# The forget gate of a hybrid decoder block: one accumulation for two blocks of positions, advanced beside the second half's operands

## Chip, cores and metric

One Trainium2 chip, one core of it. The metric is device time in microseconds (us) for one launch of the whole layer; lower is better. The core's engines are TensorE (PE, with its weight loads shown apart as PEld), VectorE (DVE), ScalarE (ACT), GpSimd (POOL) and SyncE (SP), which issues the DMAs. Each engine executes its own list of instructions strictly in order.

## What is computed

One layer over 2048 positions of width 1024, in float32. The part that the change touches is the low-rank forget gate of the gated linear attention (GLA):

```python
h = rmsnorm(x, norm1_g)
proj = h @ w_in                                  # 3088 columns
p_q, p_k, p_v, p_g, p_a, c_b, c_c, c_h = split(proj)
gate_logits = p_a @ w_gate_up + b_gate           # p_a: 16 columns, w_gate_up: 16 x 256
log_a = log_sigmoid(gate_logits) / 16
o = gla_chunked(q, k, v, log_a)                  # chunked, with a recurrent state
o = rmsnorm(o, gla_norm_g) * silu(p_g)
o_conv = c_b * causal_conv3(c_c * c_h)
x = x + concat([o, o_conv]) @ w_out
x = x + (silu(h2 @ w_ffn_gate) * (h2 @ w_ffn_up)) @ w_ffn_down      # h2 = rmsnorm(x)
out = rmsnorm(x, norm_f_g)
```

## The kernel before

**Blocks and halves.** The 2048 positions are four blocks of 512; two blocks make a half. Nearly all matrix work goes by half, as Strassen-Winograd products: the operand of a half is a 2 x 2 arrangement (rows of the width 1024 in two halves of four tiles of 128, columns the two blocks of positions), with the seven operands `B11, T1, T2, B21, T3, B22, T4` of `PRODUCTS`. `B11` and `B21` are the two width halves of the first block, `B22` is the second width half of the second block, and `T1 = B12 - B11`, so that `B11 + T1` is the first width half of the second block.

**Split numbers.** Each float32 operand is split into a high and a low part (`split`, lines 145 to 147: a copy on ACT writes the rounded high part, a subtraction on DVE the low part), and a product takes three matmuls (`product_step`, lines 334 to 336). A `unit` (line 340) is seven products of 4 x 3 matmuls on one weight tile. For it, `unit_weights` builds seven weight quarters `wq` (seven splits, four POOL operations, four buffers). Three of its accumulators are copied out by ACT (`copied`, line 354) and three products are added on DVE (`plus`, line 358).

**Input projection.** `in_proj(half)` runs twelve units: four for k, q and v, two for the output gate (their results go through Silu on ACT, line 390), six for the convolution. For the first half the first unit is done apart, by `build_first`, while the operands are being built.

**Background work.** After each product `tick` is called. While `hurry` is set, each tick takes a `step` of the list `background`; otherwise every second tick does, and of the others every second one takes a step of `ahead`, if there is one. Before, the first half's background is, in this order: `gate_weights`, six pauses, `row_stats(2)`, `row_stats(3)`, `gate(0)`, then `unhurried`, which ends the hurry, and `h1_ahead`, which makes the second half's split operands (`h` on DVE, `t` on POOL, `hi` on ACT, `lo` on DVE, stores `si...`). `gla_half(0)` is appended after the Silu units. These calls say in which order the work is written down; a scheduler then places the instructions of each engine by its own estimate of when each is ready, so what an engine really executes is the list in the built program.

**The gate before.** `gate(half)` computes the 16 gate columns for each block apart: 16 matmuls for the first block (`B11`, `B21`: two operands, four tiles, high and low) and 24 for the second (`B11`, `T1`, `B22`), line 517, each into a bank `a_ps` of its own that ACT copies to `a_sb` (line 523). `forget_gate` then does, for each of two halves of the 256 gate columns, a float32 matmul `z` (line 533), Abs on ACT (538), a DVE operation (539), Exp and Ln on ACT (540, 541), a subtraction and four scans on DVE (542, 545), two small Exp on ACT (548, 550), a subtraction on DVE (549) and a store to `s_d`, which `gla_load` reads.

**ACT's function tables.** Exp and Ln come from one table set, Silu from another. A change of set is an instruction of its own on ACT, ACT_TABLE_LOAD. The kernel asks for the set with both Exp and Ln at the start (line 988) and in `gla_half` (line 601, ordered behind the last Silu). Elsewhere a load is put in by the compiler, ahead of an activation whose function the set in place does not have.

Of the kernel before, what the change touches and what calls it, by code (L numbers as in the profile page):

```python
# [10 lines left out]
F32 = mybir.dt.float32  # L11
F32R = mybir.dt.float32r
U32 = mybir.dt.uint32
AF = mybir.ActivationFunctionType
# [33 lines left out]
def tile_hymba_block(ctx, tc, x, xt, win, wa, wgu, wout, wffn, wdown, wdown_first, small, out):  # L48
# [33 lines left out]
    dve.memset(eps[:], EPS)  # L82
    sml = const.tile([P, N_SMALL], F32, name="sml")
    nc.sync.dma_start(sml[:], small)
    wgu_sb = mixer.tile([P, 256], F32, name="wgu_sb")
    wa_sb = mixer.tile([P, (KD + 1) * 64], F32R, name="wa_sb")
    dve.memset(wa_sb[:, KD * 64 :].bitcast(F32), 0.0)
    scores = mixer.tile([P, HEADS, P], F32, name="scores")
    dve.memset(scores[:], 0.0)
    carry = mixer.tile([P, HEADS, P], F32, name="carry")  # L90
# [34 lines left out]
    def col(c):  # L125
        return sml[:, c : c + 1]

    def bank(name="mm"):
        return ps.tile([P, PB], F32, name=name, tag="mm")
# [4 lines left out]
    def bt(name, shape=(P, PB)):  # L134
        return bx[0].tile(list(shape), F32, name=name, tag="b")

    def load(dst, src):
        return nc.sync.dma_start(dst, src)

    def store(dst, src):  # L140
        return nc.sync.dma_start(dst, src)
# [3 lines left out]
    def split(src, hi, lo):  # L145
        last_hi[:] = [act.activation(hi, src, AF.Copy)]  # L146
        return dve.tensor_tensor(lo, src, hi.bitcast(F32), ALU.subtract)  # L147
# [46 lines left out]
    def unhurried():  # L194
        hurry.clear()
        yield

    def pause(n):
        for _ in range(n):
            yield  # L200
# [194 lines left out]
    def row_stats(b):  # L395
        ssq = mtiny.tile([P, PT, 2], F32, name="ssq", tag="ssq")

        def fetch(t):
            xs = [bt("xn") for _ in range(2)]
            for e, xn in enumerate(xs):  # L400
                r0 = b * PB + t * P
                load(xn[:], x[r0 : r0 + P, e * PB : (e + 1) * PB])
            return xs

        nxt = fetch(0)
        yield
        for t in range(PT):
            xs = nxt
            if t + 1 < PT:
                nxt = fetch(t + 1)  # L410
            for e, xn in enumerate(xs):
                act.activation(xn[:], xn[:], AF.Square, accum_out=ssq[:, t, e : e + 1])
            yield
        dve.tensor_tensor(ssq[:, :, 0], ssq[:, :, 0], ssq[:, :, 1], ALU.add)
        rb = bt("rb2")
        act.activation(rb[:], rows_rstd(ssq)[:], AF.Copy)
        store(s_rb[b][:], rb[:])
# [45 lines left out]

    def gate_weights():

        raw = bt("wa", (P, KD, 32))
        load(raw[:], wa)
        w = wa_sb[:, 0 : KD * 64].rearrange("p (k e c) -> p k e c", e=2, c=32)
        split(raw[:], w[:, :, 0, :], w[:, :, 1, :])
        yield  # L470

    def build_h():
# [7 lines left out]
    def h1_ahead():  # L480

        rb = []
        for j in range(2):
            r = tiny.tile([P, PB], F32, name="rb2", tag="rb")
            load(r[:], s_rb[2 + j][:])
            rb.append(r)

        def put(n, k, h):
            hi, lo = [bx[0].tile([P, PB], F32R, name=e, tag="b") for e in ("hi", "lo")]
            split(h[:], hi[:], lo[:])  # L490
            for e, y in enumerate((hi, lo)):
                store(s_h1[n][k][:, e, :], y[:].bitcast(F32))

        yield from combine(lambda k, j: xt[2 + j, :, k, :], C_G1, rb, put)
# [12 lines left out]
    def gate(half, ops):  # L507


        for j, names in enumerate((("B11", "B21"), ("B11", "T1", "B22"))):  # L510
            a = bank("a_ps")
            for i, n in enumerate(names):
                k0 = 4 if n in ("B21", "B22") else 0
                for k in range(4):
                    w = wa_sb[:, (k0 + k) * 64 : (k0 + k) * 64 + P]
                    for e in range(2):
                        pe.matmul(  # L517
                            a[:], w, ops[n][k][:, e, :], start=(i, k, e) == (0, 0, 0),
                            stop=i == len(names) - 1 and k == 3 and e == 1,
                            skip_group_check=True,  # L520
                        )
            a_sb = bt("a_sb")
            act.activation(a_sb[:], a[:], AF.Copy)
            yield
            yield from forget_gate(2 * half + j, a_sb)

    def forget_gate(b, a_sb):
        em, dn, el = [
            mtiny.tile([P, 2, PT], F32, name=n, tag=n, bufs=4) for n in ("em", "dn", "el")
        ]  # L530
        for i in range(2):
            z = bank("z")
            pe.matmul(
                z[:], wgu_sb[0:64, i * P : (i + 1) * P], a_sb[0:64, :], start=True, stop=True
            )
            bg = col(C_BG + i)
            t1, t2 = bt("g1"), bt("g2")
            act.activation(t1[:], z[:], AF.Abs, bias=bg)
            dve.tensor_scalar(t2[:], z[:], bg, 0.0, ALU.add, ALU.min)
            act.activation(t1[:], t1[:], AF.Exp, scale=-1.0)  # L540
            act.activation(t1[:], t1[:], AF.Ln, bias=one_t)
            dve.tensor_tensor(t2[:], t2[:], t1[:], ALU.subtract)
            for t in range(PT):
                s = slice(t * P, (t + 1) * P)
                dve.tensor_tensor_scan(t1[:, s], ones[:], t2[:, s], 0.0, ALU.mult, ALU.add)
            bs = t1.rearrange("p (a b) -> p a b", b=P)
            dd = t2.rearrange("p (a b) -> p a b", b=P)
            act.activation(em[:, i, :], bs[:, :, 63], AF.Exp, scale=1.0 / 16.0)
            dve.tensor_tensor(dd, bs, bs[:, :, 63:64].to_broadcast([P, PT, P]), ALU.subtract)
            act.activation(el[:, i, :], dd[:, :, P - 1], AF.Exp, scale=1.0 / 16.0)  # L550
            dve.tensor_tensor(dn[:, i, :], em[:, i, :], el[:, i, :], ALU.mult)
            store(s_d[b][i][:], t2[:])
            yield
        decays[b] = em, dn, el

    def in_proj(half, ops, first):
        def units():
# [103 lines left out]
    def gla_outputs(b, t, kq, kt, v, g):  # L661
        first = b == 0 and t == 0
        _, dn, el = decays[b]
        o = ps.tile([P, HEADS, P], F32, name="o_ps", tag="mm")
        for h in range(HEADS):
            pe.matmul(o[:, h, :], scores[:, h, :], v[:, h, :], start=True, stop=first)
            if not first:
                pe.matmul(o[:, h, :], kq[:, 2 + h // 2, :], carry[:, h, :], start=False, stop=True)
        if b < NB - 1 or t < PT - 1:
            kv = ps.tile([P, 2, P], F32, name="kv", tag="mm")  # L670
            for i in range(2):
                for e in range(2):
                    pe.matmul(
                        kv[64 * e : 64 * e + 64, i, :], kt[:, i, 64 * e : 64 * e + 64],
                        v[:, 2 * i + e, :], start=True, stop=True,
                    )
            for i in range(2):
                last = el[:, i, t : t + 1]
                if first:
                    dve.tensor_scalar(state[i][:], kv[:, i, :], last, None, ALU.mult)  # L680
                else:
                    kvs = mtiny.tile([P, P], F32, name="kvs", tag="kvs")
                    dve.tensor_scalar(kvs[:], kv[:, i, :], last, None, ALU.mult)
                    dve.scalar_tensor_tensor(
                        state[i][:], state[i][:], dn[:, i, t : t + 1], kvs[:], ALU.mult, ALU.add
                    )
        ssq, l, y0 = [mtiny.tile([P, HEADS], F32, name=n, tag=n) for n in ("hsq", "hl", "hy")]
        sq = mtiny.tile([P, P], F32, name="sq", tag="rep")
        for h in range(HEADS):
            act.activation(sq[:], o[:, h, :], AF.Square, accum_out=ssq[:, h : h + 1])  # L690
        dve.tensor_scalar(ssq[:], ssq[:], 1.0 / P, EPS, ALU.mult, ALU.add)
        rsqrt(ssq[:], ssq[:], l[:], y0[:])
        osb = bt("osb", (P, HEADS, P))
        rs = ssq[:].rearrange("p (h c) -> p h c", c=1).to_broadcast([P, HEADS, P])
        dve.tensor_tensor(osb[:], o[:], rs, ALU.mult)
        return osb, g
# [237 lines left out]
    def last_unit(src, ops, b12, y, ssq):  # L934
# [49 lines left out]
        for j in range(2):  # L984
# [2 lines left out]

    act.preload_act_table_set("natural_log_exp_and_others")
    first_loads()
    load(wgu_sb[:], wgu)  # L990
    ops, first = build_h()
    hurry.append(True)
    background.extend(
        [
            gate_weights(), pause(6), row_stats(2), row_stats(3), gate(0, ops), unhurried(),
            h1_ahead(),
        ]
    )
    in_proj(0, ops, first)
    drain_background(lambda: len(background) < 2)  # L1000
    ops = load_pairs(s_h1)
    background.append(gate(1, ops))
# [121 lines left out]
```

## Time and profile before

| | |
|---|---|
| median of 3 runs | 2141.64 us (2137.0 to 2144.77) |
| the profiled execution | 2147.18 us, of which its span is 2145.4 us |
| mean granted TensorE clock | 0.983 of full speed |
| busy, share of the span | PE 96%, PEld 77%, DVE 67%, ACT 47%, POOL 46% |
| first half's gate matmuls (line 517) | 118 to 136 us |
| first half's Silu | 155 to 191 us |
| second half's gate matmuls | from 472 to 503 us |

Times in the views are microseconds from the start of the span. A row of a timeline gives start, duration, engine, line, operation, output and inputs, count, and in brackets the idle time of the engine just before it with what ended that. A row of groups gives count, busy time, mean nanoseconds of one, and the idle time before them. Rows of windows give busy time and instruction count of each engine in a stretch. Neighbouring instructions of one engine overlap a little in the records, so a duration is somewhat longer than the distance to the next start.

### The profile page before, as it was taken

The page shows a single profiled execution, that of the slowest core. Times are in us where ns is not written, and L with a number is a line of the kernel's source. Part 1 is how long each engine was busy: PE and PEld are TensorE (multiplying, and loading weights), DVE is VectorE, ACT ScalarE, POOL GpSimd, SP SyncE. Part 2 cuts the span into 40 slices and gives each one's busy share as a digit, 9 for nine tenths or more (in the row PEclk, how much of TensorE's full clock was granted, in tenths as well). Part 3 has the DMA queues.
Part 4 walks back from the last instruction along what each step waited for, and adds up shares of the span by engine and source line. Part 5 has one row for each costly group of instructions (what it writes and reads, how often), then busy time and mean ns, then how long its engine had stood idle before and what let it go on. Part 6 is the DMA issues. An engine that isn't in the chain of part 4 may idle for free.

```text
span 2145.4 us, 26958 instructions
## 1 busy us (share of the span) xinstructions
PE 2052.6 (96%) x9137; PEld 1658.6 (77%) x9137; DVE 1438.1 (67%) x2035; ACT 1008.4 (47%) x1961; POOL 983.5 (46%) x707
## 2 busy tenths in 40 slices
PE   6899899999999999999999999999999999999996
PEld 4677787887788887788888887787888888887774
DVE  7668975548664496688887674654686677664554
ACT  6455345564544334554555453333464454553344
POOL 3425422221201374555655436774644654435773
PEclk9899999999999999999999999999999999999998
DMA  7348667432486982466454577688455455587662
GB/s 270 125 145 296 225 267 249 154 121 88 154 305 190 348 295 103 167 246 220 181 226 177 208 303 266 257 333 351 155 199 210 148 188 196 186 334 275 265 265 108
DMA packets 191563, 471.85 MB, mean 220 GB/s; under 512 B 20032, under 2 KB 65344, under 8 KB 181824
## 3 DMA queue, kind: packets, MB, share of 16 engines
q1 hardware_dynamic: 191424, 470.12, 60.5%
q8 instruction: 72, 1.18, 0.2%
q14 instruction: 67, 0.55, 0.1%
HBM read 301.22 MB, written 168.82 MB: 219 GB/s over the span
## 4 chain that ended last, share of the span: by engine, by line
PE 73%; DMA 10%; DVE 10%; issue 3%; ACT 3%; POOL 1%; SPq 0%; DVEq 0%; ACTq 0%; POOLq 0%
PE mm L334 21%; PE mm L336 21%; PE mm L335 21%; DVE wq L147 2%; PE mm L742 2%; PE mm L745 2%; PE mm L743 2%; DMA raw<-in_wdown_dram 1%; DVE op L147 1%; DMA op<-sa_B 1%; DVE h L460 1%; DMA op<-shT 1%; DMA raw<-in_wffn_dram 1%; PE a_ps L517 1%; DVE so L147 1%
## 5 line engine op out<-in xcount | busy, mean ns | idle before, releaser
L334 PE MATMUL mm<-op,wq 128*128 128x512 f32 x2495 | 987.4, 398 | 31.1 <-ACT c L354 17.0
L336 PE MATMUL mm<-op,wq 128*128 128x512 f32 x2495 | 971.7, 394 | 19.6 <-DVE wq L147 18.8
L335 PE MATMUL mm<-op,wq 128*128 128x512 f32 x2495 | 979.0, 392 | 2.6 <-DVE op L147 2.6
L147 DVE TENSOR_TENSOR wq<-raw,wq 128x512 fp32r<-128x512 f32 (+2 forms) x628 | 532.2, 852 | 306.7 <-ACT wq L146 304.9
L146 ACT ACTIVATE wq<-raw 128x512 fp32r<-128x512 f32 (+2 forms) x628 | 367.7, 589 | 582.1 <-PE mm L336 416.0
L334 PEld LDWEIGHTS mm<-op,wq 128*128 128x128 f32 x2495 | 473.2, 190 | 151.2 <-ACT c L354 22.9
L336 PEld LDWEIGHTS mm<-op,wq 128*128 128x128 f32 x2495 | 473.1, 190 | 129.9 <-DVE wq L147 30.4
L335 PEld LDWEIGHTS mm<-op,wq 128*128 128x128 f32 x2495 | 473.9, 190 | 102.2 <-DVE op L147 4.3
L319 POOL TENSOR_TENSOR raw<-s,raw 128x512 f32<-128x512 f32 (+2 forms) x98 | 130.8, 1335 | 439.2 <-DVE wq L147 391.2
L358 DVE TENSOR_TENSOR c<-mm,c 128x512 f32<-128x512 f32 x270 | 185.3, 686 | 121.7 <-PE mm L336 119.6
L317 POOL TENSOR_TENSOR s<-raw 128x512 f32<-128x512 f32 (+2 forms) x98 | 128.5, 1311 | 196.5 <-DMA raw<-in_wffn_dram 92.2
L324 POOL TENSOR_TENSOR raw<-raw 128x512 f32<-128x512 f32 (+2 forms) x98 | 128.6, 1313 | 144.6 <-DVE wq L147 119.5
L354 ACT ACTIVATE c<-mm 128x512 f32<-128x512 f32 x270 | 156.6, 586 | 27.6 <-PE mm L336 27.0
L724 POOL TENSOR_TENSOR ssx<-ssx,q 128x512 f32<-128x512 f32 x52 | 74.6, 1447 | 152.8 <-ACT q L723 152.7
L318 POOL TENSOR_TENSOR raw<-raw 128x512 f32<-128x512 f32 (+2 forms) x98 | 138.5, 1414 | 4.5
L904 POOL TENSOR_TENSOR y<-c,y 128x512 f32<-128x512 f32 x66 | 99.3, 1506 | 68.4 <-DVE c L358 68.2
L146 ACT ACTIVATE wq<-s 128x512 fp32r<-128x512 f32 (+2 forms) x98 | 57.7, 589 | 103.3 <-PE mm L336 101.1
L147 DVE TENSOR_TENSOR so<-t,so 128x512 fp32r<-128x512 f32 x100 | 89.5, 902 | 23.5 <-ACT so L146 23.4
L742 PE MATMUL mm<-op,wq 128*128 128x512 f32 x256 | 100.7, 394 | 0.0
L743 PE MATMUL mm<-op,wq 128*128 128x512 f32 x256 | 99.8, 390 | 0.0
L147 DVE TENSOR_TENSOR wq<-s,wq 128x512 fp32r<-128x512 f32 (+2 forms) x98 | 87.0, 888 | 15.7 <-ACT wq L146 15.1
L146 ACT ACTIVATE so<-t 128x512 fp32r<-128x512 f32 x100 | 62.7, 629 | 48.4 <-DMA sa_B<-so 22.5
(173 smaller groups left out, 1893.1 us busy)
## 6 DMA issues: line engine op xcount, KB each, us to landing
raw<-in_wffn_dram SPq DMA_DIRECT2D x44, 1024.0 KB, 5.9
sa_T<-so SPq DMA_DIRECT2D x88, 512.0 KB, 4.6
op<-sa_T SPq DMA_DIRECT2D x88, 512.0 KB, 9.6
sa_B<-so SPq DMA_DIRECT2D x69, 512.0 KB, 3.4
op<-sa_B SPq DMA_DIRECT2D x69, 512.0 KB, 9.5
raw<-in_win_dram SPq DMA_DIRECT2D x23, 1024.0 KB, 5.7
raw<-in_wdown_dram SPq DMA_DIRECT2D x24, 768.0 KB, 6.2
sx<-y SPq DMA_DIRECT2D x48, 256.0 KB, 4.8
```

The costliest lines, as they stand in the source:

```text
L146: last_hi[:] = [act.activation(hi, src, AF.Copy)]
L147: return dve.tensor_tensor(lo, src, hi.bitcast(F32), ALU.subtract)
L318: pool.tensor_tensor(a21, a11, a21, ALU.subtract)
L319: pool.tensor_tensor(a11, s1, a11, ALU.subtract)
L324: pool.tensor_tensor(a12, a12, a11, ALU.subtract)
L334: pe.matmul(o[:], wh, xh, start=first and k == 0, stop=False, skip_group_check=True)
L335: pe.matmul(o[:], wh, xl, start=False, stop=False, skip_group_check=True)
L336: return pe.matmul(o[:], wl, xh, start=False, stop=k == n - 1, skip_group_check=True)
L354: act.activation(t[:], o[:], AF.Copy)
L358: dve.tensor_tensor(t[:], o[:], t[:], ALU.add)
L742: pe.matmul(o[e, j][:], wh, m[:, 0, :], start=k == 0, stop=False)
L743: pe.matmul(o[e, j][:], wh, m[:, 1, :], start=False, stop=False)
```

## The change

`gate` accumulates both blocks in one bank: the weight columns of the first block are put in output rows 0 to 31 and those of the second in rows 32 to 63, with zero columns where an operand belongs to one block alone. So one chain of 32 matmuls (`B11`, `T1`, `B21`, `B22`, each four tiles, high and low) and one copy `a_sb` replace 40 matmuls and two copies per half. `wa_sb` grows to 23 x 32 columns with its zeros, and is filled by three splits of 4 x 16 columns in place of one of 8 x 32. The two `z` matmuls of a pair contract over 32 rows each, rows 0 to 31 and rows 32 to 63, into two banks. `wgu_sb` has 64 rows, loaded by four DMAs in place of one. `kvs` in the GLA gets one buffer in place of two. The first half's `gate(0)` leaves the hurried background and becomes `ahead`: it takes one step at every fourth tick, from the end of the hurry on, while `h1_ahead` starts where the gate had stood. The second half's gate stays where it was in the background.

```diff
-    wgu_sb = mixer.tile([P, 256], F32, name="wgu_sb")
-    wa_sb = mixer.tile([P, (KD + 1) * 64], F32R, name="wa_sb")
-    dve.memset(wa_sb[:, KD * 64 :].bitcast(F32), 0.0)
+    wgu_sb = mixer.tile([64, 256], F32, name="wgu_sb")
+    wa_sb = mixer.tile([P, 23 * 32], F32R, name="wa_sb")
+    dve.memset(wa_sb[:].bitcast(F32), 0.0)
...
     def gate_weights():
...
-        w = wa_sb[:, 0 : KD * 64].rearrange("p (k e c) -> p k e c", e=2, c=32)
-        split(raw[:], w[:, :, 0, :], w[:, :, 1, :])
+        top = wa_sb[:, 0 : 12 * 32].rearrange("p (k e c) -> p k e c", e=6, c=16)
+        low = wa_sb[:, 12 * 32 : 20 * 32].rearrange("p (k e c) -> p k e c", e=4, c=16)
+        r0, r1 = raw[:, 0:4, 0:16], raw[:, 4:8, 0:16]
+        split(r0, top[:, :, 2, :], top[:, :, 3, :])
+        split(r0, top[:, :, 4, :], top[:, :, 5, :])
+        split(r1, low[:, :, 2, :], low[:, :, 3, :])
         yield
...
     def gate(half, ops):
-        for j, names in enumerate((("B11", "B21"), ("B11", "T1", "B22"))):
-            a = bank("a_ps")
...
-            a_sb = bt("a_sb")
-            act.activation(a_sb[:], a[:], AF.Copy)
-            yield
-            yield from forget_gate(2 * half + j, a_sb)
+        a = bank("a_ps")
+        names = "B11", "T1", "B21", "B22"
+        for n in names:
+            for k in range(4):
+                q = {"B11": 3 * k + 1, "T1": 3 * k, "B21": 2 * k + 13, "B22": 2 * k + 12}[n]
+                w = wa_sb[:, 32 * q : 32 * q + P]
+                for e in range(2):
+                    pe.matmul(
+                        a[:], w, ops[n][k][:, e, :], start=(n, k, e) == ("B11", 0, 0),
+                        stop=n == "B22" and k == 3 and e == 1, skip_group_check=True,
+                    )
+        a_sb = bt("a_sb")
+        act.activation(a_sb[:], a[:], AF.Copy)
+        yield
...
         for i in range(2):
...
+            zs = [bank("z") for _ in range(2)]
+            for j in range(2):
+                r = slice(32 * j, 32 * j + 32)
+                pe.matmul(
+                    zs[j][:], wgu_sb[r, i * P : (i + 1) * P], a_sb[r, :], start=True, stop=True
+                )
+            for j in range(2):
+                forget_gate(2 * half + j, i, zs[j], *small[j])
+                yield
...
-                    kvs = mtiny.tile([P, P], F32, name="kvs", tag="kvs")
+                    kvs = mtiny.tile([P, P], F32, name="kvs", tag="kvs", bufs=1)
...
-    load(wgu_sb[:], wgu)
+    for i in range(4):
+        load(wgu_sb[16 * i : 16 * i + 16, :], wgu[0:16, :])
     ops, first = build_h()
     hurry.append(True)
     background.extend(
         [
-            gate_weights(), pause(6), row_stats(2), row_stats(3), gate(0, ops), unhurried(),
-            h1_ahead(),
+            gate_weights(), pause(6), row_stats(2), row_stats(3), unhurried(), h1_ahead(),
         ]
     )
+    ahead.append(gate(0, ops))
     in_proj(0, ops, first)
+    for _ in ahead.pop():
+        pass
     drain_background(lambda: len(background) < 2)
```

The operations inside `forget_gate` are the same as before; it is called once for each block and each half of the gate columns, in the new order.

More of the change, by code (lines that the diff above doesn't have):

```diff
@@ L507, in gate @@
     def gate(half, ops):
-        for j, names in enumerate((("B11", "B21"), ("B11", "T1", "B22"))):
-            a = bank("a_ps")
[L512 to L521, printed above, removed]
-            a_sb = bt("a_sb")
-            act.activation(a_sb[:], a[:], AF.Copy)
-            yield
-            yield from forget_gate(2 * half + j, a_sb)
@@ L527, in forget_gate @@
[L527 to L530, printed above, removed]
-        for i in range(2):
[L532 to L554, printed above, removed]
@@ new lines, in gate @@
+        a_sb = bt("a_sb")
+        act.activation(a_sb[:], a[:], AF.Copy)
+        yield
+        small = {}
+        for j in range(2):
+            small[j] = decays[2 * half + j] = [
+                mtiny.tile([P, 2, PT], F32, name=n, tag=n, bufs=4) for n in ("em", "dn", "el")
+            ]
+        for i in range(2):
+            zs = [bank("z") for _ in range(2)]
[4 more added lines that the diff above has]
+                )
+            for j in range(2):
+                forget_gate(2 * half + j, i, zs[j], *small[j])
+                yield
@@ new lines, in forget_gate @@
+    def forget_gate(b, i, z, em, dn, el):
+        bg = col(C_BG + i)
+        t1, t2 = bt("g1"), bt("g2")
+        act.activation(t1[:], z[:], AF.Abs, bias=bg)
+        dve.tensor_scalar(t2[:], z[:], bg, 0.0, ALU.add, ALU.min)
+        act.activation(t1[:], t1[:], AF.Exp, scale=-1.0)
+        act.activation(t1[:], t1[:], AF.Ln, bias=one_t)
+        dve.tensor_tensor(t2[:], t2[:], t1[:], ALU.subtract)
+        for t in range(PT):
+            s = slice(t * P, (t + 1) * P)
+            dve.tensor_tensor_scan(t1[:, s], ones[:], t2[:, s], 0.0, ALU.mult, ALU.add)
+        bs = t1.rearrange("p (a b) -> p a b", b=P)
+        dd = t2.rearrange("p (a b) -> p a b", b=P)
+        act.activation(em[:, i, :], bs[:, :, 63], AF.Exp, scale=1.0 / 16.0)
+        dve.tensor_tensor(dd, bs, bs[:, :, 63:64].to_broadcast([P, PT, P]), ALU.subtract)
+        act.activation(el[:, i, :], dd[:, :, P - 1], AF.Exp, scale=1.0 / 16.0)
+        dve.tensor_tensor(dn[:, i, :], em[:, i, :], el[:, i, :], ALU.mult)
+        store(s_d[b][i][:], t2[:])
```

## The prediction

> **What bounds the kernel now.** I read the page first: is one engine the bound?
>
> ```profile
> span 2145.4 us, 26958 instructions
> PE 2052.6 (96%) x9137; PEld 1658.6 (77%) x9137; DVE 1438.1 (67%) x2035; ACT 1008.4 (47%) x1961; POOL 983.5 (46%) x707
> ```
>
> TensorE is the bound as an average: a matmul removed is time removed, and work on an engine half busy should be free. But the change moves work within one stage, so I next cut the first half's input projection into windows (and, for comparison, a stretch of the second half's, 424 to 463 us). Columns: stretch, length, then busy time and count of PE, PEld, DVE, ACT, POOL, granted clock, DMA share and rate.
>
> ```profile
> 110.00:149.10 39.10, 38.62 (x160) 28.67 (x159) 22.93 (x52) 20.35 (x42) 5.17 (x4) 1.00 0.33 116
> 149.10:194.80 45.70, 41.20 (x171) 32.61 (x170) 41.95 (x46) 25.36 (x45) 26.84 (x16) 0.96 0.86 294
> 194.80:260.00 65.20, 58.27 (x245) 46.44 (x244) 63.43 (x87) 29.27 (x54) 33.18 (x20) 0.97 0.74 244
> 424.00:463.00 39.00, 39.00 (x214) 32.17 (x212) 20.94 (x40) 29.90 (x57) 10.72 (x8) 1.00 0.46 153
> ```
>
> The first stretch is where the gate stands now: PE loses 0.5 us of 39, and DVE and ACT have over 16 us to spare each. From 149 us on, when `h1_ahead` has begun, DVE is over 90% busy and PE loses 4.5 us of 45.7, then 6.9 of 65.2. The waits of TensorE from 149.1 to 260 us say for whom:
>
> ```profile
> PE mm L334 <- ACT c L354: 8.0, 5, 3.0
> PE mm L336 <- DVE wq L147: 3.3, 3, 1.8
> ```
>
> TensorE waits for ScalarE's copies of accumulators and for the splits of weights. ACT's own list is therefore on the path here, though ACT is 47% busy overall. The change puts the first half's gate just into this stretch, between Silu's.
>
> **Matmuls removed.** Rows of TensorE's timelines (start, duration, count), and last a row of the tile `sc` (smallest, median, largest duration in ns):
>
> ```profile
> 472.37 2.72 PE L517 MATMUL a_ps<-op,wa_sb 128*128 128x512 f32 x11
> 497.78 5.76 PE L517 MATMUL a_ps<-op,wa_sb 128*128 128x512 f32 x24
> 125.63 1.98 PE L533 MATMUL z<-a_sb,wgu_sb 64*128 64x512 f32 x4 [0.48 <-ACT a_sb L523]
> 138.82 1.12 PE L533 MATMUL z<-a_sb,wgu_sb 64*128 64x512 f32 x2
> 317.50 0.71 PE L642 MATMUL sc<-kq 64*128 64x128 f32 x8
> 318.42 0.60 PE L651 MATMUL v_ps<-ident,vt 128*128 128x128 f32 x4
> L642 PE MATMUL sc<-kq x40: 272/272/373, 297.5 to 383.2; 64*128 64x128 f32 x40
> ```
>
> 24 gate matmuls take 5.76 us and 11 take 2.72, so each further one takes 3.04 / 13 = 0.234 us. (A product of twelve takes 2.8 us.) Each half drops 8: 1.9 us per half. A `z` is two passes; four take 1.98 us and two 1.12, so they come 0.43 apart. Whether the pair on rows 0 to 31 and 32 to 63 overlaps, the trace of before doesn't show for 512 columns. The nearest rows: eight `sc` passes, which alternate two row groups, come (0.71 - 0.27) / 7 = 0.06 us apart, four full-height `v_ps` passes of the same width (0.60 - 0.27) / 3 = 0.11. So one overlap of 0.43 us per pair at best, nothing at worst, where the two stand together. In the built program three of the four pairs do. I take the better end for the second half's two pairs, -0.9 us, since the `sc` row is the same kind of pair. In the first half the `z` lie in a stretch that ACT will pace (below), and give nothing.
>
> **The first half's gate on ScalarE.** What decides is the built program's list of ACT instructions. Before, from the first Silu to the `gla_half` load of tables, it holds 11 weight splits and two table loads. In the changed program the four `forget_gate` calls lie between the Silu's, each Silu takes the table away, each Exp and Ln fetches one again (not one with both), and the same list holds **20 table loads** (42 against 24 in the whole program). What one costs:
>
> ```profile
> 148.54 0.64 ACT L146 ACTIVATE wq<-raw 128x512 fp32r<-128x512 f32 x1 [0.37 <-PE mm L336]
> 149.08 0.58 ACT L354 ACTIVATE c<-mm 128x512 f32<-128x512 f32 x1
> ...
> 193.51 1.28 ACT L601 ACT_TABLE_LOAD   x1
> 194.80 0.63 ACT L146 ACTIVATE hi<-h 128x512 fp32r<-128x512 f32 x1
> ...
> 443.70 1.65 ACT L658 ACTIVATE carry<-state,em 64x128 f32<-64x128 f32 x4
> 445.37 1.28 ACT L151 ACT_TABLE_LOAD   x1
> 446.67 0.21 ACT L151 ACTIVATE hl<-hsq 128x4 f32<-128x4 f32 x1
> ```
>
> A load takes 1.28 us; the activation ahead of it ends 0.02 us before (445.35), the one behind starts 0.02 us after. The Trainium skill, "ScalarE: Activation LUTs", section "What ACT_TABLE_LOAD costs", has 1.283 us for the load, as here, and a further drain of 1.38 us for each switch. The trace disagrees on the drain: it shows no such gap. By that page 18 more loads would be an estimated 47.9 us of ACT, and the sum below 24.8 us larger.
>
> By the rows, 18 more loads are 18 x 1.283 = 23.1 us of ACT.
>
> Now the stretch from the first Silu load to the end of the `gla_half` load, as the changed program lists it: 13 weight splits, 12 `hi`, 6 copies `c`, 8 Silu, the 20 activations of four gates, 20 loads. Durations from ACT's groups, 110 to 194.8 us:
>
> ```profile
> L146 ACT ACTIVATE wq<-raw 128x512 fp32r<-128x512 f32 x20 | 12.6, 629 | 3.8 <-PE mm L336 3.4 <-POOL raw L319 0.2
> L354 ACT ACTIVATE c<-mm 128x512 f32<-128x512 f32 x11 | 6.4, 591 | 2.5 <-PE mm L336 2.5
> L390 ACT ACTIVATE c<-c 128x512 f32<-128x512 f32 x6 | 3.8, 634 | 3.6 <-DVE c L358 3.6
> L541 ACT ACTIVATE g<-g,ones 128x512 f32<-128x512 f32 x4 | 2.9, 724 | 0.1
> L538 ACT ACTIVATE g<-z,sml 128x512 f32<-128x512 f32 x4 | 2.7, 684 | 0.7 <-PE z L533 0.7
> L540 ACT ACTIVATE g<-g 128x512 f32<-128x512 f32 x4 | 2.5, 630 | 0.1
> L390 ACT ACT_TABLE_LOAD x1 | 1.3, 1283 | 0.0
> L550 ACT ACTIVATE el<-g 128x4 f32<-128x4 f32 x4 | 0.8, 204 | 1.0 <-DVE g L549 1.0
> ```
>
> 13 x 0.63 + 12 x 0.63 + 6 x 0.59 + 8 x 0.63 + 4 x (0.68 + 0.63 + 0.72 + 2 x 0.20) + 20 x 1.28 = 59.7 us. Where no load stands between them neighbours overlap by 0.1 us (148.54 to 149.08 is 0.54 for a row of 0.64): 39 such places take off 3.9. So 55.8 to 59.7, I take 57.8 us of pure ACT work.
>
> Before, the same 13 weight splits (the ones after 149.08, up to the load that ends at 194.8) took 45.7 us, with 25.4 of ACT work and 20.3 of ACT waiting. In the changed kernel the stretch can start earlier by what TensorE no longer does ahead of it: 1.9 us for eight matmuls, 4.0 for the eight `z` passes that come later. So it starts at 149.1 - 5.9 = 143.2 and ends at 143.2 + 57.8 = 201.0 if ACT never waits: 6.2 us late already. How much it waits is the large unknown. DVE brings 42 us of its own work in the stretch and gets the gate's on top:
>
> ```profile
> L545 DVE TENSOR_TENSOR_SCAN g<-ones,g 128x128 f32<-128x128 f32 x16 | 5.6, 407 | 0.1
> L539 DVE TENSOR_SCALAR g<-z,sml 128x512 f32<-128x512 f32 x4 | 3.0, 746 | 1.6 <-ACT g L538 1.6
> L549 DVE TENSOR_TENSOR g<-g 128x512 f32<-128x512 f32 x4 | 2.8, 688 | 0.0
> L542 DVE TENSOR_TENSOR g<-g,g 128x512 f32<-128x512 f32 x4 | 2.7, 683 | 0.7 <-ACT g L541 0.7
> ```
>
> That is 14.1 more, 56 us, as much as ACT has; and the two wait on each other (`hi` then `lo`, Ln then scans, scans then Exp). Ends: no wait and the shorter sum (143.2 + 55.8 = 199.0, 4.2 late), or all 20.3 us of before (143.2 + 57.8 + 20.3 = 221.3, 26.5 late). A third of the old waiting, 7.2 us, is my choice: an engine that is itself late seldom waits, but DVE is as late. So the stretch is 65 us, and ACT **13.4 us late**.
>
> Does TensorE lose as much? Queued behind the late instructions are weight splits and copies `c`, and TensorE waits for both. Four `wq` buffers let it lag, but between the product whose accumulator is copied and the one that needs the copy stands one product only. So it hides 0 to 2.8 us, I take half, -1.4. Nothing gives the rest back: after this stretch the lists hold nearly the same work as before (15 `hi` are through, against 14).
>
> **The rest.** The larger memset of `wa_sb` (736 columns) runs in DVE's first microseconds, which wait for the first loads: nothing. Two more small splits of `wa`, and three more tiny loads on SP: nothing to +0.5 us, taken as nothing, while TensorE there waits for operands. `kvs` with one buffer: written and read by DVE alone, in order: nothing. Two copies `a_sb` fewer: off the path. SP: the gate's stores are moved among `h1_ahead`'s stores and weight loads; in the new list one weight load stands behind two of them, the next behind the other two. They are due a unit early; a rival if not.
>
> **The sum**, against the profiled execution (span 2145.4, its time 2147.2, which is 5.5 above the median of 2141.6; I apply the difference to the median): 13.4 - 1.4 - 1.9 (second half's matmuls) - 0.9 (`z`) = **+9.2 us: 2156.4 for that execution, 2150.8 for the median.** Ends: 4.2 - 2.8 - 1.9 - 0.9 = -1.4 (2140.2), and 26.5 - 1.9 = +24.6 (2166.2). About 0.3%, 6.4 us, is what can be told from no change, so "same" is 2135.2 to 2148.1. Chance of this case 0.62, most of it slower (0.50).
>
> **Rivals.** (1) *The loads hide; not slower.* In the stretch at 424 us seven table loads pass while TensorE loses nothing (39.00 of 39.00), with ACT 77% busy. If the changed stretch too ends by 194.8 us, only the savings stay: -(16 x 0.234 + 3 x 0.43) = -5.0, 2136.6 us. It would need ACT to do its 55.8 us within 51.6 from 143.2, so it decides there whether other stretches lend time (TensorE lagging, or loads falling into waits already counted). Against: 57.8 is ACT work alone. Chance 0.22, a quarter of it faster.
> (2) *The smoothing works, and the next stretch gains too.* `h1_ahead` is one `hi` further by 194.8; if that freed DVE, the 6.9 us lost up to 260 would go: -5.0 - 6.9 = -11.9, 2129.7 us. Against: one split. Chance 0.07.
> (3) *Each load also holds ACT for as long again.* 18 x 1.28 = +23.1: 2173.9 us. Against: rows 443.70 to 446.67. Chance 0.03. This is what the drain in "ScalarE: Activation LUTs" of the Trainium skill would do.
> (4) *SP compounds it.* A late gate store holds SP, so the weight load behind it is late and ACT waits. SP's waits, 110 to 195 us:
>
> ```profile
> SPq L141 <- DVE g L549: 16.0, 4, 9.0
> ```
>
> SP already stood up to 9.0 us for one gate result. Two such holds on a weight load: +18 on the forecast, 2168.8 us. Chance 0.06.
>
> **How the numbers follow.** The likeliest is 2150.8. Below 2135 lie rival 2 and a little of rival 1, above 2167 rivals 3 and 4: about 0.2 left out, so 2135 to 2167. Faster 0.06 + 0.07 = 0.13; same 0.16 + 0.12 = 0.28; slower 0.50 + 0.03 + 0.06 = 0.59.
>
> **What would show it.** Right: some 18 ACT_TABLE_LOAD more, 1.28 us each; a stretch between first Silu load and the `gla_half` load of about 65 us with ACT about 90% busy; more waiting of `mm` for `c` and `wq` there; 16 fewer `a_ps`. Wrong: that stretch at 55 us or less, or TensorE losing no more than 5 us in it; or a loss that lies after 260 us.

## The result and the profile after

The changed kernel takes 2146.9 us (median of 12 runs, 2143.86 to 2150.67), the kernel before 2140.69 (12 runs). The ratio is 1.0031, 95% interval 1.0021 to 1.0041: 4.5 to 8.8 us slower, 6.6 in the middle.

The page of the changed kernel, its first lines:

```profile
span 2145.0 us, 26919 instructions
PE 2048.3 (95%) x9121; PEld 1656.0 (77%) x9121; DVE 1437.4 (67%) x2037; ACT 1026.8 (48%) x1979; POOL 981.6 (46%) x707
```

TensorE has 4.3 us less to do and ACT 18.4 more. The profiled execution of before lay 6 us above its median (2147.18 us), so the two spans say nothing of the change; the stages do. The windows of the changed kernel, cut at the first Silu load and at the end of the `gla_half` load (same columns as before):

```profile
110.00:143.98 33.98, 33.98 (x149) 26.98 (x148) 19.18 (x30) 13.54 (x29) 11.55 (x8) 1.00 0.51 166
143.98:201.69 57.71, 46.11 (x176) 33.63 (x176) 45.44 (x70) 55.45 (x79) 21.18 (x14) 0.94 0.59 207
201.69:268.60 66.91, 59.70 (x248) 46.56 (x246) 64.34 (x85) 28.49 (x53) 31.01 (x19) 0.97 0.71 246
```

In the middle stretch ACT is busy 55.45 of 57.71 us, where it had been 25.4 of 45.7, and TensorE loses 11.6 us, where it had lost 4.5. Rows of ACT's timeline from its beginning and end:

```profile
143.98 1.28 ACT L390 ACT_TABLE_LOAD   x1
145.27 0.63 ACT L390 ACTIVATE c<-c 128x512 f32<-128x512 f32 x1
145.81 0.67 ACT L550 ACTIVATE g<-z,sml 128x512 f32<-128x512 f32 x1
146.50 1.28 ACT L552 ACT_TABLE_LOAD   x1
147.79 0.63 ACT L552 ACTIVATE g<-g 128x512 f32<-128x512 f32 x1
148.33 0.61 ACT L146 ACTIVATE hi<-h 128x512 fp32r<-128x512 f32 x1
148.96 1.28 ACT L553 ACT_TABLE_LOAD   x1
150.26 0.72 ACT L553 ACTIVATE g<-g,ones 128x512 f32<-128x512 f32 x1
...
200.41 1.28 ACT L611 ACT_TABLE_LOAD   x1
```

One Silu, a load, Exp, a load, Ln: where the kernel doesn't ask for the joint set itself, the two functions of one gate fetch a table each. ACT's only wait in the whole stretch for another engine that the view of waits names, and TensorE's waits from 143.98 to 262 us:

```profile
ACT L560 <- DVE g L557: 1.7, 2, 1.1
```

```profile
PE mm L334 <- ACT c L354: 9.1, 5, 3.9
PE mm L334 <- ACT wq L146: 3.8, 4, 1.6
PE mm L336 <- DVE wq L147: 2.4, 2, 2.2
PE mm L334 <- DVE c L358: 2.2, 1, 2.2
```

Before, TensorE waited 8.0 us for ACT there (149.1 to 260 us); now 12.9. As a mark for the end of the first half I use the first `sc` matmuls of the GLA, which have the same 876 matmuls of units ahead of them in both kernels. The rows of before and after:

```profile
297.54 0.72 PE L642 MATMUL sc<-kq 64*128 64x128 f32 x8
```

```profile
306.10 0.71 PE L652 MATMUL sc<-kq 64*128 64x128 f32 x8
```

The first half ends 8.6 us later. The second half gives something back. Its gate on TensorE, two more rows of before (the `z` row stands there four times) and then the rows of after:

```profile
477.68 1.32 PE L517 MATMUL a_ps<-op,wa_sb 128*128 128x512 f32 x5
484.39 1.12 PE L533 MATMUL z<-a_sb,wgu_sb 64*128 64x512 f32 x2
```

```profile
481.63 2.73 PE L524 MATMUL a_ps<-op,wa_sb 128*128 128x512 f32 x11
486.97 5.06 PE L524 MATMUL a_ps<-op,wa_sb 128*128 128x512 f32 x21
497.43 1.13 PE L540 MATMUL z<-a_sb,wgu_sb 32*128 32x512 f32 x4
506.87 1.13 PE L540 MATMUL z<-a_sb,wgu_sb 32*128 32x512 f32 x4
```

2.73 + 5.06 + 2 x 1.13 = 10.1 us in place of 2.72 + 1.32 + 5.76 + 4 x 1.12 = 14.3: 4.2 us saved. 8.6 - 4.2 = +4.4 us, just below the measured interval. (In a second profile of the kernel before the mark is at 299.03 us; by that one the sum is 7.1 - 4.2 = +2.9.)

### The profile page after: what moved, and what is told of

Its sections match the earlier page's. It is cut to its first block, busy times and chain, and to the rows that moved or that the text cites. A ratio compares the mean times of both kernels' runs of the same rounds, so it can differ in the third digit from the quotient of the medians.

```text
span 2145.0 us, 26919 instructions
## 1 busy us (share of the span) xinstructions
PE 2048.3 (95%) x9121; PEld 1656.0 (77%) x9121; DVE 1437.4 (67%) x2037; ACT 1026.8 (48%) x1979; POOL 981.6 (46%) x707
## 4 chain that ended last, share of the span: by engine, by line
PE 73%; DVE 10%; DMA 7%; ACT 5%; issue 3%; POOL 1%; SPq 1%; DVEq 0%; ACTq 0%; POOLq 0%
PE mm L334 22%; PE mm L336 21%; PE mm L335 21%; DVE wq L147 2%; PE mm L752 2%; PE mm L753 2%; PE mm L755 2%; DMA raw<-in_wdown_dram 1%; DVE op L147 1%; DVE h L460 1%; DMA op<-sa_B 1%; ACT wq L146 1%; DVE so L147 1%; PE o_ps L676 1%; SPq L138 1%
## 5 line engine op out<-in xcount | busy, mean ns | idle before, releaser
L147 DVE TENSOR_TENSOR wq<-s,wq 128x512 fp32r<-128x512 f32 (+2 forms) x98 | 82.0, 837 | 16.8 <-ACT wq L146 16.3
```

## The experiments

**Theory A**: the table loads fill ACT's list, and TensorE, which needs ACT's copies and splits, follows. **Rival B**: the gate's own work beside `h1_ahead` crowds that stretch, loads or not. **Rival C**: the merged gate itself costs the time. The results, each against runs of the kernel before on the same chip; us is (ratio - 1) x 2141, and `sc` the start of the mark in the profile. The intervals reach 2 to 5 us to each side, so two rows that lie 2 us apart aren't told apart.

| kernel | table loads | ratio (95%) | us | `sc` at |
|---|---|---|---|---|
| before | 24 | 1 | 0 | 297.54; 299.03 in a second profile |
| changed | 42 | 1.0031 (1.0021 to 1.0041) | +6.6 | 306.10 |
| merged bank, old place | 26 | 0.9979 (0.9967 to 0.9991) | -4.5 | 297.10 |
| new place, two banks | 34 | 1.0043 (1.0029 to 1.0058) | +9.2 | 307.34 |
| changed, no loads in the gate | 24 | 0.9989 (0.9977 to 1.0001) | -2.4 | 295.56 |
| changed, no Ln | 36 | 1.0005 (0.9994 to 1.0016) | +1.1 | 303.46 |
| new place, two banks, no loads | 24 | 1.0020 (1.0006 to 1.0035) | +4.3 | 301.03 |
| changed, every second tick | 34 | 0.9989 (0.9978 to 1.0) | -2.4 | 300.28 |
| merged bank, no pauses | 25 | 0.9935 (0.9913 to 0.9957) | -13.9 | 289.26 |
| before, no pauses | 24 | 1.0015 (1.0003 to 1.0027) | +3.2 | 299.28 |
| changed, no pauses | 30 | 0.9961 (0.9948 to 0.9973) | -8.4 | (`gla_half` begins earlier) |

**Merged bank, old place.** The gate goes back into the hurried background:

```diff
-            gate_weights(), pause(6), row_stats(2), row_stats(3), unhurried(), h1_ahead(),
+            gate_weights(), pause(6), row_stats(2), row_stats(3), gate(0, ops), unhurried(),
+            h1_ahead(),
...
-    ahead.append(gate(0, ops))
...
-    for _ in ahead.pop():
-        pass
```

> One bank for both blocks, with the first half's gate back in its old place in the hurried background (2 table loads more than before, against 18 more in the changed kernel). Theory A (the table loads put between the Silu's delay ScalarE, and TensorE with it) and rival B (the gate's work itself crowds the stretch of h1_ahead, loads or not) both expect faster than before: 16 gate matmuls x 0.234 = 3.7 us and four pairs of z at half their time, 4 x 1.05 = 4.2 us, less 2 loads: about 2133 to 2136 us. Rival C (the loss comes from the merged gate itself: zero columns, 32-row tiles, larger splits) expects about 2147 us, as the changed kernel.

Measured 2139.18 us, -4.5. Rival C falls: the merged gate is a gain, though a smaller one than A and B expected. It is about that of the second half alone (4.2): in the first half the mark moves by 0.4 us only (1.9 by the second profile of before), although TensorE has 4 us less to do there. One wait takes them back: TensorE stands 4.7 us for DVE's part of a weight split. In this half, whose later stretch DVE and ACT pace, fewer matmuls were worth next to nothing.

**New place, two banks.** The same three edits the other way round, on the kernel before.

> Two banks and the old matmuls, but the first half's gate taken from the background and advanced at every fourth tick, as in the change (10 table loads more than before). Theory A: ACT's stretch is 10 x 1.28 us shorter in loads than the one with 18, so ACT is at most some 3 us late, and nothing is saved: 2141 to 2147 us. Rival B: the same work crowds the same stretch, and none of the 8 us of the merged bank is saved: 2150 to 2155 us. Rival C: 2140 us, as before.

Measured 2151.43 us, +9.2: what rival B expected, and more than theory A. So A isn't all of it. The windows show where (from the first Silu load to the `gla_half` load, and on to 300 us):

```profile
143.44:194.00 50.56, 45.91 (x180) 34.58 (x179) 33.36 (x52) 38.89 (x56) 18.43 (x12) 0.93 0.55 196
194.00:205.00 11.00, 10.45 (x46) 8.32 (x45) 9.46 (x19) 7.46 (x17) 2.20 (x1) 1.00 0.71 253
205.00:300.00 95.00, 83.40 (x342) 66.61 (x341) 79.52 (x112) 36.55 (x67) 43.02 (x26) 0.95 0.58 194
```

ACT gets through by 194.0, no later than before, but TensorE loses 4.7 us there and 11.6 more from 205 to 300 (before: 6.9 in that window).

**The changed kernel without the loads.** This is the cleanest of the runs: the lists of instructions are the same on every engine but for 18 table loads.

```diff
+        exp, small = (AF.Copy, 1.0 / 4096.0) if b < 2 else (AF.Exp, 1.0 / 16.0)
...
-        act.activation(t1[:], t1[:], AF.Exp, scale=-1.0)
-        act.activation(t1[:], t1[:], AF.Ln, bias=one_t)
+        act.activation(t1[:], t1[:], exp, scale=-1.0)
+        if b < 2:
+            act.activation(t1[:], t1[:], AF.Abs, bias=one_t)
+        else:
+            act.activation(t1[:], t1[:], AF.Ln, bias=one_t)
...
-        act.activation(em[:, i, :], bs[:, :, 63], AF.Exp, scale=1.0 / 16.0)
+        act.activation(em[:, i, :], bs[:, :, 63], exp, scale=small)
...
-        act.activation(el[:, i, :], dd[:, :, P - 1], AF.Exp, scale=1.0 / 16.0)
+        act.activation(el[:, i, :], dd[:, :, P - 1], exp, scale=small)
```

> The changed kernel with its order of instructions kept on every engine, but the first half's gate uses Copy and Abs in place of Exp and Ln, so that no table load is needed there (24 loads in the program, as before, against 42); the decays of the first half are therefore not computed. Theory A: ACT's stretch from first Silu load to the gla_half load falls from 57.7 us to about 45 or less, the lateness goes and the savings of the merged bank stay: 2133 to 2138 us. Rival B: DVE's crowding stays, 2144 to 2147 us. Rival C: 2147 us.

Measured 2139.69 us, -2.4, against +6.6 with the loads. The window from the Silu load to the `gla_half` load, and the mark:

```profile
142.42:191.38 48.96, 43.48 (x177) 31.43 (x176) 45.28 (x69) 32.57 (x61) 20.64 (x14) 1.00 0.72 251
```

```profile
295.56 0.72 PE L656 MATMUL sc<-kq 64*128 64x128 f32 x8
```

The stretch is 48.96 us in place of 57.71 and the mark comes 10.5 us earlier; ACT has 32.6 us of work, what is left of 55.45 without 18 loads. DVE's 45.3 us of work are the same as with loads (45.4). So 18 loads, 23.1 us of ACT, cost 9.0 us of time (6.6 + 2.4). That is theory A, for the changed kernel, though the time lies 1.7 us above the range that A gave. A part of the loss is not waiting: the granted clock in the stretch is 1.00 without the loads and 0.94 with them. From 143 to 300 us of the changed kernel's trace 19 matmuls of the units start 0.43 us after the one ahead, not 0.23, against 6 without the loads: some 2.5 of the 10.5 us.

**The changed kernel without Ln**, 12 loads more than before.

```diff
-        act.activation(t1[:], t1[:], AF.Ln, bias=one_t)
+        act.activation(t1[:], t1[:], AF.Abs if b < 2 else AF.Ln, bias=one_t)
```

> The changed kernel with its order kept, but the first half's gate takes Abs in place of Ln, so that Exp alone needs a table (36 loads, 12 more than before); the logarithm of the first half is left out. Theory A: 6 loads fewer, up to 7.7 us off ACT's stretch of 57.7: 2139 to 2143 us, between the changed kernel and the one without loads. Rivals B and C: 2146 to 2147 us.

Measured 2143.79 us, +1.1, between the two as A expected. Its window from the first Silu load to the end of the `gla_half` load:

```profile
145.11:198.90 53.79, 44.25 (x176) 32.50 (x175) 46.14 (x70) 47.59 (x73) 21.17 (x14) 0.97 0.64 225
```

Over 0, 12 and 18 extra loads ACT's waiting in the stretch goes 16.4, 6.2, 2.3 us: most of the loads fall into waits that were there. Whether the last six cost more apiece than the first twelve isn't shown. By the times they cost 5.5 and 3.5 us, each with an uncertainty of 3 us or more; by the mark, of one profile each, 2.6 and 7.9.

**New place, two banks, without the loads**: the same substitution on the move alone.

> The move alone (two banks, gate at every fourth tick) with its order kept and Copy and Abs in place of Exp and Ln in the first half's gate, so that its 10 extra table loads go; the decays of the first half are not computed. Its parent was 9 us slower than before, more than theory A expected for 10 loads. Theory A, loads: 2140 to 2143 us, most of the 9 us gone. Rival B, the gate's work: 2148 to 2151 us, the 9 us stay.

Measured 2145.11 us, +4.3. Both were half right: 4.9 of the 9.2 us are the loads, 4.3 remain without any. From 205 to 300 us TensorE still loses 10.8:

```profile
205.00:300.00 95.00, 84.23 (x348) 66.78 (x347) 77.31 (x111) 36.45 (x66) 39.47 (x24) 0.96 0.58 195
```

So the gate's work in this place costs too, when the gate has two banks and is finished late. TensorE's waits in that window are 5.8 us for ACT's copies `c` and 3.6 for sums on DVE (before: 4.4 and none); what makes these late I haven't taken apart.

**The changed kernel, a step at every second tick.**

```diff
-        elif ahead and pace[0] % 4 == 1:
+        elif ahead and (pace[0] % 4 == 1 or pace[0] < 30):
```

> The changed kernel with the first half's gate advanced at every second tick in place of every fourth, so that more of it is done ahead of the Silu's: 10 table loads more than before, against 18. Theory A (loads delay ScalarE): ACT's stretch carries 10 us fewer of loads and 5 us less of gate; the first half ends at most 2 us behind before, and with 4.6 us saved in the second half the time is 2136 to 2141 us. Rival B (crowding by the gate's own work in the stretch of h1_ahead): the first half ends some 8 us late as in the changed kernel, 2145 to 2148 us.

The edit gives the gate every odd tick of the first 29. Measured 2140.17 us, -2.4. The gate is beside the operands, as in the change, but two of its four parts have their Exp and Ln ahead of the first Silu load, where the changed kernel has none, and the loss is gone: A's number, not B's.

**Merged bank, old place, no pauses.**

```diff
-            gate_weights(), pause(6), row_stats(2), row_stats(3), gate(0, ops), unhurried(),
+            gate_weights(), row_stats(2), row_stats(3), gate(0, ops), unhurried(),
```

> The merged bank with the gate in its old place, and the six pauses ahead of row_stats taken out, so that the gate and h1_ahead begin six ticks (some 16 us) earlier, in the stretch where DVE is half idle. If DVE's load from 150 to 260 us sets TensorE's idle time there (11 us), the first half ends 2 to 5 us earlier than with the merged bank alone: 2133 to 2136 us. If TensorE's stalls there come from the convolution's work and not from h1_ahead, the time is that of the merged bank alone, about 2138.

Measured 2127.81 us, -13.9: faster than both kernels, and by more than expected; the mark comes 7.8 us before that of the merged bank alone. First the window from 110 to 143 us and the first `hi` of `h1_ahead` in the merged bank alone, then both in this kernel:

```profile
110.00:143.00 33.00, 32.93 (x145) 25.48 (x144) 18.84 (x40) 17.61 (x38) 6.87 (x4) 1.00 0.37 130
```

```profile
140.64 0.63 ACT L146 ACTIVATE hi<-h 128x512 fp32r<-128x512 f32 x1 [0.22 <-DVE h L460]
```

```profile
110.00:143.00 33.00, 29.06 (x124) 21.74 (x123) 32.46 (x52) 19.16 (x39) 13.87 (x9) 1.00 0.59 197
```

```profile
125.77 0.64 ACT L146 ACTIVATE hi<-h 128x512 fp32r<-128x512 f32 x1 [1.04 <-DVE h L460]
```

`h1_ahead` begins 15 us earlier and DVE does 32.5 us of work there in place of 18.8. What that is worth shows behind it, from 143 to 260 us; the kernel before, the merged bank alone, and this kernel:

```profile
143.00:260.00 117.00, 105.57 (x437) 83.50 (x438) 111.41 (x146) 59.10 (x107) 60.02 (x36) 0.97 0.76 253
```

```profile
143.00:260.00 117.00, 103.20 (x423) 82.35 (x422) 112.13 (x146) 59.94 (x105) 58.93 (x36) 0.94 0.74 254
```

```profile
143.00:260.00 117.00, 110.42 (x480) 89.00 (x479) 101.22 (x132) 56.95 (x101) 57.14 (x37) 1.00 0.71 245
```

TensorE loses 11.4, 13.8 and 6.6 us there, and the granted clock is full only in the last. The edit moves the gate too, its matmuls to 94 to 118 us; this run doesn't part the two.

**The kernel before and the changed kernel, both without pauses.** The same edit.

> The kernel before without its six pauses: gate and h1_ahead six ticks earlier, two banks, 24 table loads. The merged bank without pauses was 14 us faster than before, the merged bank alone 4.5. If the two effects add, this one is 2131 to 2133 us, 8 to 10 us faster; if the pauses matter only together with the merged bank, 2138 to 2142 us.

Measured 2145.12 us, +3.2: neither expectation. Without the merged bank the pauses' removal is no gain. The profile shows that it does less of the same thing: the first `hi` comes at 138.28 us, not 125.77 (147.54 in the kernel before), and DVE does 23.4 us of work from 110 to 143, not 32.5:

```profile
110.00:143.00 33.00, 31.12 (x130) 23.57 (x129) 23.39 (x43) 15.66 (x33) 5.88 (x4) 1.00 0.36 123
```

```profile
138.28 0.62 ACT L146 ACTIVATE hi<-h 128x512 fp32r<-128x512 f32 x1
```

That is still 9 us earlier than before, and from 143 to 260 us TensorE loses 9.2 us in place of 11.4. But from 110 to 143 it had lost 1.9 in place of 0.5, and done 130 matmuls in place of 136. Why the one outweighs the other stays open.

> The changed kernel without the six pauses: the gate in the idle ticks is then mostly done before the Silu's, and 6 table loads are left over of the 18 more. Theory A (half a microsecond per load, and the rest the crowding of DVE) expects 2130 to 2134 us, some 3 us behind the merged bank without pauses. If the place beside h1_ahead is bad in itself, loads or not, it expects 2137 us or more.

Measured 2132.57 us, -8.4, as A expected, 5.5 us behind the merged bank without pauses, with six loads more than the kernel before (ten between the first Silu load and the `gla_half` load, where that kernel has two). The changed kernel's place for the gate is thus not bad in itself; it is bad where the Silu's are. The first `hi` comes at 114.59 us here, 11 us ahead of the faster kernel's, so an early start of the operands isn't all that counts either.

**The kernel before, once more**, for its profile.

> The kernel before once more, for a second profile. In the first one the work between 770 and 910 us ran some 8 us behind every other profile taken so far, also behind kernels whose instructions there are the same. If that is a difference between executions, this profile shows those 8 us gone and a time near 2139 us; if it belongs to the kernel before, they are there again.

One execution, 2146.73 us; the slow work was there again, and both profiled executions of before lie 5 to 6 us over its median. But between the 109th and the 261st weight split on ACT they take 592.8 and 591.7 us, while the two kernels with the gate moved and two banks, whose instructions there are the same, take 587.4 and 584.9. So it isn't the instructions; what it is stays open. It is why stages after 300 us are not compared with the profile of before above, except row by row.

## Why the prediction was right, step by step

**The table loads** were right in number and price: 42 in the program, 1.28 us each, the next activation 0.01 us behind. No drain shows (143.98 + 1.28 = 145.26, and Silu starts at 145.27): rival 3 falls. With it falls, for this kernel, the drain that the Trainium skill states in "ScalarE: Activation LUTs", section "What ACT_TABLE_LOAD costs".

**The stretch on ACT.** Begin 143.2 forecast, 143.98 measured; pure work 57.8 forecast (55.8 to 59.7), 55.45 measured; end 208.2 forecast (201.0 without any waiting), 201.69 measured. The term that failed is the waiting: 7.2 us forecast, 2.3 measured (57.71 - 55.45). DVE was not "as late": it had 45.4 us of work there, not 56. The gate's part was larger than forecast, 20.1 us against 14.1, but DVE's own was 25 in place of 42: it made 5 `h` and not 9, and the same subtractions took less. Before (149.1 to 194.8 us) and after (the stretch):

```profile
L147 DVE TENSOR_TENSOR wq<-raw,wq 128x512 fp32r<-128x512 f32 x12 | 12.6, 1051 | 1.5 <-ACT wq L146 1.4
L147 DVE TENSOR_TENSOR lo<-h,hi 128x512 fp32r<-128x512 f32 x8 | 9.8, 1219 | 1.0 <-ACT hi L146 1.0
```

```profile
L147 DVE TENSOR_TENSOR wq<-raw,wq 128x512 fp32r<-128x512 f32 x12 | 8.9, 744 | 1.5 <-ACT wq L146 1.5
L147 DVE TENSOR_TENSOR lo<-h,hi 128x512 fp32r<-128x512 f32 x8 | 6.5, 817 | 3.9 <-ACT hi L146 3.4 <-ACT em L560 0.4
```

Fewer of them met an operation of POOL, which had less to do in the stretch (21.2 us against 26.8). In both traces the subtractions of line 147 with no POOL operation beside them took 0.68 us; with one they took 1.38 on average before and 0.89 after. Before, 17 of 28 had one beside them; after, 9 of 26. So ACT was 6.9 us late, not 13.4.

**What TensorE hides.** 1.4 us forecast; none is seen. By the first profile of before ACT is 6.9 us late and the mark 8.6; by the second, whose stretch ends at 196.2, they are 5.5 and 7.1.

**The second half.** 2.8 us forecast, 4.2 measured. The matmuls were right, the `z` pair under-sized: it saves 1.1 us, not 0.43 (last section).

The sum was +9.2, the measured change +6.6 (4.5 to 8.8). Its path was right: loads, then ACT, then TensorE's waits. That the sum came as near is partly luck, since its errors had opposite signs: ACT's lateness was 6.5 us too large (4.9 of waiting, 2.4 of work, less 0.8 for the later begin), the second half's gain 1.4 too small, and the mark lost 1.7 more than ACT in place of 1.4 less. With the measured terms it is 6.9 + 1.7 - 4.2 = +4.4, or +2.9 by the second profile. The 2 to 4 us from there to the middle of the interval stay open. Rival 1 falls at the mark: 201.69, not 194.8; "seven loads without a loss" was a stretch with ACT 77% busy, and this one would have had to be over 100%. Rival 2 falls in the changed kernel: the third window still loses 7.2 us. The merged bank without pauses shows a gain of that kind, 6.6 us lost in place of 13.8. Rival 4: SP's waits for a gate result from 110 to 205 us were at most 2.0 us, not 9.0, and no wait of ACT for weights is named. SP was not the cause:

```profile
SPq L141 <- DVE g L561: 4.3, 3, 2.0
```

## To carry to other kernels

An engine that is half busy on average can be full in the stretch to which work is moved: add up that engine's list there, from the built program, with the table loads that the new neighbours force. Work that needs one activation table should not be spread among work that needs another: the same gate at every second tick, half of it done ahead of the Silu's, was no slower than before. And the idle time worth filling was on DVE ahead of the crowded stretch, not on TensorE: with the merged bank, beginning the gate and the second half's operands earlier was worth another 9.4 us beside its 4.5. With two banks the same edit was worth nothing, so this is a thing to try, not a rule.

## What had not been expected of the hardware

Two float32 `z` of 32 rows each, in two row groups and two banks, take together as long as one did: four passes in 1.13 us against two passes of 64 rows in 1.12. The `sc` rows had suggested a gain of less than half. And 18 table loads, 23.1 us of ACT's time, cost 9.0 us of the kernel's: ACT had waited 16.4 us in the stretch without them and waited 2.3 with them.
